# Depthwise taps of four channel blocks as shifted matmuls over (token parity, channel), the other four on VectorE, in a hybrid encoder trunk

## The chip, the core and the metric

One Trainium2 core runs the whole program; the other cores are idle. Its engines run side by side and meet at semaphores: TensorE (PE; its weight loads are listed apart as PEld), VectorE (DVE), ScalarE (ACT), GpSimd (POOL) and SyncE (SP), which issues the DMAs. The metric is device microseconds of one execution, lower is better. The kernel before was timed three times: 1600.88, 1602.43 and 1603.56 us, median 1602.43.

## What is computed

A trunk of four layers over one sequence of 256 tokens of 1024 channels, all in float32. Each layer has a token mixer (retention, Conformer convolution, dilated attention, retention again) and then a SwiGLU channel mixer, each between RMSNorms with a residual. The change touches the convolution mixer of layer 1:

```python
def _conv_mixer(h, w_in, b_in, w_dw, b_dw, ln_g, ln_b, w_out, b_out):
    a = h @ w_in + b_in
    u = a[..., :D_MODEL] * jax.nn.sigmoid(a[..., D_MODEL:])
    u = lax.conv_general_dilated(
        u, w_dw[:, None, :], window_strides=(1,), padding=[(15, 15)],
        dimension_numbers=('NWC', 'WIO', 'NWC'), feature_group_count=D_MODEL) + b_dw
    u = jax.nn.silu(_layernorm(u, ln_g, ln_b))
    return u @ w_out + b_out
```

The convolution is depthwise: each channel has its own 31 taps over time, and no channel sees another.

## The kernel before

The tokens lie in two tiles of 128 (t = 0, 1), the channels in eight blocks of 128 (cb). The order of the tokens within the tiles is a permutation that the host applies to input, masks and tables and takes back at the end: position p holds token 4 * (p mod 64) + p // 64, so each tile holds two of the four residues modulo 4.

Large products are split into a high and a low float32r part of both operands (`split`, L49: a cast on ACT, L50, and a subtraction on DVE, L51) and summed over three single-pass matmuls. Weights come in by SP's queue into one of seven `raw` buffers (`load_w`, L62, L64) and are split into `wh` and `wl` there. A buffer comes free when its reader has finished, and SP issues its DMAs in program order.

The convolution mixer (`conv`, L514) runs in these stages:

- `glu(t, c, ...)`: 24 matmuls of a projection (L183), scaled out of PSUM by ACT (`cab`, L534), transposed on TensorE to channels by tokens (L537), a sigmoid on ACT (L541), and the gating product on DVE (L544), which writes the tokens in their natural order into `upad`, 15 zeros on either side. It is called for (0,0), (0,1), (1,0), (0,2), (1,1), (0,3), (1,2), (1,3); call c gives the channel blocks 2c and 2c + 1.
- `taps(cb)`: the 31 taps of a block. By the table PE_TAPS, blocks 0, 2, 4 and 6 are done on DVE as one scaling (L559) and 30 multiply-adds over 256 tokens (L561). Blocks 1, 3 and 5 are done on TensorE: ACT builds a diagonal matrix for each tap (`dg`, L574), and an f32 matmul of 256 columns adds the shifted `upad` into a PSUM bank (L577). Of block 7 TensorE does seven taps and adds DVE's part of the rest through an identity (L585). ACT adds the bias and puts the tokens back in permuted order (`cvp`, L587).
- LayerNorm: transposes back to tokens by channels (L617), statistics (L620, L621), a reciprocal root on POOL (L112, L113), normalisation half on DVE (`yc`, L625) and half on ACT (L626), transposes (L634), affine and SiLU on ACT (`sy`, L637), and a split into `yh` and `yl`.
- The output product with conv_w_out (L200). Its first three weight blocks are split right behind the last tap on DVE (the `issue_after` at L605).

A scheduler places each instruction on its engine from an estimate of when its inputs will be there, so the order on an engine is not the order of the code.

## Time and profile before

| | |
|---|---|
| median of the three runs | 1602.43 us |
| the profiled execution's own time | 1601.92 us |
| its span, first to last instruction | 1600.1 us |
| PE busy | 1579.5 us, 99% of the span |
| DVE busy | 1046.6 us, 65% |
| ACT busy | 870.4 us, 54% |
| POOL busy | 71.7 us, 4% |
| moved by DMA | 274.27 MB, mean 171 GB/s |
| granted TensorE clock | 0.997 of full speed |

A row of a timeline gives the start, the length, the engine, the line of the kernel, the operation, output and inputs, how many instructions are merged, and in brackets the idle time before it and what ended it. The length of a merged row runs from its first start to its last end. An f32 matmul that accumulates shows as two instructions, so 100 of them count x200; transposes and float32r matmuls are one. Matmuls are pipelined, so one lasts longer than the distance to the next; that distance (the pitch) is what a stream costs. Line numbers are those of the kernel before unless said otherwise.

### The profile page before, as it was taken

The numbers are of one execution on the slowest core, as the hardware profiler recorded it, in microseconds if no ns is written. First come the engines' busy times: TensorE is split into PE (matmuls) and PEld (weight loads), VectorE is DVE, ScalarE is ACT, GpSimd is POOL, SyncE is SP. The second block draws the span as 40 slices with busy tenths as digits, with TensorE's granted clock in tenths as the row PEclk, the third lists the DMA queues.
The fourth block names the chain that finished last, engine by engine and source line by source line (L and its number), as shares of the span: only waits on it lengthen the run. The fifth ranks groups of instructions, "written<-read, shape, count | busy, mean of one in ns | idle before, by whom it ended". The sixth has DMA issues, their size and how long they took to land.

```text
span 1600.1 us, 21034 instructions
## 1 busy us (share of the span) xinstructions
PE 1579.5 (99%) x7742; PEld 1342.0 (84%) x7742; DVE 1046.6 (65%) x1594; ACT 870.4 (54%) x1392; POOL 71.7 (4%) x106
## 2 busy tenths in 40 slices
PE   9999999999999999999999999999999999999998
PEld 6888878888787888889999999888888888878886
DVE  7755684556697855467777877845567655675452
ACT  7544464545677654446666666745456444555441
POOL 1000010001000200010000000100010000010000
PEclk9999999999999999999999999999999999999999
DMA  8645475555303755444454444665655554576530
GB/s 314 231 139 192 148 241 189 189 206 180 127 1 132 263 177 210 156 139 159 130 155 151 148 146 159 214 207 175 209 179 168 183 168 131 163 237 202 193 119 27
DMA packets 79881, 274.27 MB, mean 171 GB/s; under 512 B 9377, under 2 KB 9633, under 8 KB 79778
## 3 DMA queue, kind: packets, MB, share of 16 engines
q1 hardware_dynamic: 79778, 272.92, 51.1%
q8 instruction: 61, 1.00, 0.3%
q14 instruction: 42, 0.34, 0.1%
HBM read 271.84 MB, written 1.05 MB: 171 GB/s over the span
## 4 chain that ended last, share of the span: by engine, by line
PE 89%; ACT 3%; DVE 3%; DMA 2%; issue 1%; POOL 1%; SPq 0%; DVEq 0%; POOLq 0%; ACTq 0%
PE mm L183 56%; PE acc L200 20%; PE acc L577 3%; PE acc L776 1%; PE aux L459 1%; PE aux L324 1%; ACT wh L50 1%; PE aux L761 1%; DMA raw<-in_ffn_w_out 1%; PE acc L735 1%; DMA raw<-in_ffn_w_in 1%; ACT junk L118 1%; DMA raw<-in_ret_w_in 1%; DVE wl L51 1%; PE acc L733 1%
## 5 line engine op out<-in xcount | busy, mean ns | idle before, releaser
L183 PE MATMUL mm<-wh,xTh 128*128 128x512 f32 (+1 forms) x1536 | 591.0, 385 | 1.1 <-ACT xTh L50 1.1
L183 PE MATMUL mm<-wh,xTl 128*128 128x512 f32 (+1 forms) x1536 | 579.3, 377 | 0.0
L183 PE MATMUL mm<-wl,xTh 128*128 128x512 f32 (+1 forms) x1536 | 579.2, 377 | 0.0
L51 DVE TENSOR_TENSOR wl<-raw,wh 128x1024 fp32r<-128x1024 f32 (+1 forms) x432 | 498.1, 1163 | 117.6 <-ACT wh L50 103.6
L50 ACT CAST wh<-raw 128x1024 fp32r<-128x1024 f32 (+1 forms) x432 | 429.9, 1004 | 138.8 <-PE mm L183 103.3
L183 PEld LDWEIGHTS mm<-wh,xTl 128*128 128x128 f32 x1536 | 288.6, 188 | 46.0 <-DVE xTl L51 0.3
L183 PEld LDWEIGHTS mm<-wh,xTh 128*128 128x128 f32 x1536 | 289.0, 188 | 43.3 <-ACT xTh L50 1.5
L183 PEld LDWEIGHTS mm<-wl,xTh 128*128 128x128 f32 x1536 | 289.4, 188 | 41.8 <-DVE wl L51 0.5
L448 ACT ACTIVATE fsg<-mm,rsx 128x256 f32<-128x256 f32 x88 | 41.7, 474 | 168.2 <-PE mm L183 168.2
L450 DVE SCALAR_TENSOR_TENSOR fsg<-mm,rsx,fsg 128x256 f32<-128x256 f32 x88 | 42.3, 481 | 123.6 <-ACT fsg L448 123.5
L51 DVE TENSOR_TENSOR pooll<-raw,poolh 128x1024 fp32r<-128x1024 f32 x88 | 107.3, 1222 | 7.5 <-ACT poolh L50 6.7
L200 PE MATMUL acc<-poolh,fhh 128*128 128x512 f32 x344 | 107.6, 393 | 0.5 <-ACT fhh L50 0.5
L200 PE MATMUL acc<-poolh,fhl 128*128 128x512 f32 x344 | 107.2, 392 | 0.0
L200 PE MATMUL acc<-pooll,fhh 128*128 128x512 f32 x344 | 106.0, 389 | 0.0
L50 ACT CAST poolh<-raw 128x1024 fp32r<-128x1024 f32 x88 | 92.6, 1054 | 23.7 <-PE acc L200 14.6
L51 DVE TENSOR_TENSOR fhl<-aux,fhh 128x256 fp32r<-128x256 f32 x88 | 37.1, 421 | 97.9 <-ACT fhh L50 97.9
L50 ACT CAST fhh<-aux 128x256 fp32r<-128x256 f32 x88 | 32.5, 369 | 114.8 <-PE aux L459 114.8
L200 PEld LDWEIGHTS acc<-poolh,fhh 128*128 128x128 f32 x344 | 63.7, 188 | 15.1 <-ACT fhh L50 2.7
L200 PEld LDWEIGHTS acc<-pooll,fhh 128*128 128x128 f32 x344 | 64.6, 188 | 13.5
L200 PEld LDWEIGHTS acc<-poolh,fhl 128*128 128x128 f32 x344 | 64.3, 188 | 13.5
L561 DVE SCALAR_TENSOR_TENSOR cv<-upad,wdw,cv 128x256 f32<-128x256 f32 x143 | 59.5, 478 | 0.8
L110 POOL TENSOR_SCALAR rs<-ss 128x1 f32<-128x1 f32 x16 | 7.6, 475 | 1040.5 <-ACT junk L118 1040.5
(180 smaller groups left out, 1622.0 us busy)
## 6 DMA issues: line engine op xcount, KB each, us to landing
raw<-in_ffn_w_in SPq DMA_DIRECT2D x176, 512.0 KB, 4.7
raw<-in_ret_w_in SPq DMA_DIRECT2D x96, 512.0 KB, 4.9
raw<-in_ffn_w_out SPq DMA_DIRECT2D x88, 512.0 KB, 4.7
raw<-in_attn_w_in SPq DMA_DIRECT2D x96, 384.0 KB, 3.7
raw<-in_ret_w_out SPq DMA_DIRECT2D x32, 512.0 KB, 4.5
raw<-in_conv_w_in SPq DMA_DIRECT2D x16, 512.0 KB, 4.7
gain<-in_norm_w SPq DMA_DIRECT2D x15, 512.0 KB, 5.5
raw<-in_conv_w_out SPq DMA_DIRECT2D x8, 512.0 KB, 4.5
```

The lines of the kernel that those rows point to most:

```text
L50: ia = nc.scalar.copy(h, src)
L51: iv = nc.vector.tensor_sub(l, src, h.bitcast(F32))
L118: nc.scalar.activation(junk, src, AF.Square, scale=scale, accum_out=acc)
L183: nc.tensor.matmul(out, lhsT=st[t][:, k, :], rhs=mv[:, sl], start=(n == 0), stop=(n == 23))
L200: nc.tensor.matmul(acc[hh], lhsT=st, rhs=mv[:, hh * 512 : hh * 512 + 512], start=(first and i == 0), stop=(last and i == 2),)
L324: nc.tensor.matmul(b, lhsT=pt[:, m, t * P : (t + 1) * P], rhs=vt[:, m, :], start=(n == 0), stop=(n == 5))
L448: nc.scalar.activation(sg, b[:, 0:256], AF.Silu, scale=rsx[t])
L450: nc.vector.scalar_tensor_tensor(out=sm, in0=b[:, 256:512], scalar=rsx[t], in1=sg, op0=ALU.mult, op1=ALU.mult)
L459: nc.tensor.transpose(tp[:, k * P : (k + 1) * P], sm[:, k * P : (k + 1) * P], ident)
L561: last_tap["v"] = nc.vector.scalar_tensor_tensor(out=cv, in0=upad[:, cb, w : w + 256], scalar=wdw[:, cb, w : w + 1], in1=cv, op0=ALU.mult, ...
L577: nc.tensor.matmul(pc[:, 0:256], lhsT=dgs[w], rhs=upad[:, cb, w : w + 256], start=(w == 0), stop=(w == TAPS - 1),)
L733: nc.tensor.matmul(b[:, 0:256], lhsT=x[:, 0, ts_(t)], rhs=y[:, h, :], start=(n == 0), stop=(n == 2))
```

## The change

The token order becomes by parity: position p holds token 2 * (p mod 128) + p // 128, so tile 0 holds the even tokens and tile 1 the odd ones.

Blocks 0 to 3 are all done on DVE, 31 taps each. For blocks 4 to 7 the gating product writes `su`, channels by tokens of one parity. Sixteen DMAs on POOL's queue copy halves of 64 channels into `uw`, whose 128 partitions are (token parity, 64 channels), for eight groups of 64 channels, 144 columns each, zeroed by a POOL memset. A convolution over 31 tokens is then 16 shifts by one pair of tokens: for each shift d a matmul takes the 128 columns of `uw` from d on as its stationary operand and, as its moving operand, a 128x128 matrix that maps (input parity, channel) to (output parity, channel); it holds the tap 2d + q - r on its diagonals. These matrices are made by the host (conv_tz, 8.4 MB) and come through the `raw` buffers, sixteen loads of 512 KB. The result is already tokens by channels, so these blocks aren't transposed back; their bias enters as two single-row matmuls per PSUM bank (`cbrh`, `cbrl`). The statistics are taken in four pieces of 256 channels, and ACT normalises its half in two strided pieces.

```diff
--- before.py
+++ after.py
@@ -30,8 +30,8 @@
 CONV_FENCE = 1
 APE = 3
 PTB = 1
-PE_TAPS = (0, 31, 0, 31, 0, 31, 0, 7)
-TAP_ORDER = (0, 1, 2, 3, 4, 5, 6, 7)
+VB = 4
+SHIFTS = 16
 
 
 @with_exitstack
@@ -518,14 +518,21 @@
         nc.sync.dma_start(wdw, a["conv_w_dw"][j])
         bout = pool.tile([P, D], F32, tag="cbout", name="cbout", bufs=1)
         nc.sync.dma_start(bout, a["conv_b_out"][j : j + 1, :].partition_broadcast(P))
-        upad = pool.tile([P, KB, 288], F32, tag="upad", name="upad", bufs=1)
+        brow = pool.tile([1, D], F32, tag="cbrow", name="cbrow", bufs=1)
+        nc.sync.dma_start(brow, a["conv_b_row"][j : j + 1, :])
+
+        upad = pool.tile([P, VB, 288], F32, tag="upad", name="upad", bufs=1)
         nc.vector.memset(upad[:, :, 0:15], 0.0)
         nc.vector.memset(upad[:, :, 271:288], 0.0)
-        cvp = pool.tile([P, KB, 256], F32, tag="cvp", name="cvp", bufs=1)
-
-        def perm(v):
-
-            return v.rearrange("p (u r) -> p r u", r=4)
+        cvp = pool.tile([P, VB, 256], F32, tag="cvp", name="cvp", bufs=1)
+
+        GR = 2 * (KB - VB)
+        su = pool.tile([P, KB - VB, 2, P], F32, tag="su", name="su", bufs=1)
+        uw = pool.tile([P, GR, 144], F32, tag="uw", name="uw", bufs=1)
+        nc.gpsimd.memset(uw, 0.0)
+        brh = pool.tile([1, D], F32R, tag="cbrh", name="cbrh", bufs=1)
+        brl = pool.tile([1, D], F32R, tag="cbrl", name="cbrl", bufs=1)
+        split(brh, brl, brow)
 
         def glu(t, c, ws, mid=None):
             b = bank("mm")
@@ -541,23 +548,32 @@
                 nc.scalar.activation(
                     sg, tp[:, (2 + k) * P : (3 + k) * P], AF.Sigmoid, bias=chv[:, 4, cb : cb + 1]
                 )
+                if cb < VB:
+                    dst = upad[:, cb, 15:271].rearrange("p (v t) -> p t v", t=2)[:, t, :]
+                else:
+                    dst = su[:, cb - VB, t, :]
                 nc.vector.scalar_tensor_tensor(
-                    out=perm(upad[:, cb, 15:271])[:, 2 * t : 2 * t + 2, :],
-                    in0=tp[:, k * P : (k + 1) * P].rearrange("p (r u) -> p r u", r=2),
+                    out=dst,
+                    in0=tp[:, k * P : (k + 1) * P],
                     scalar=chv[:, 3, cb : cb + 1],
-                    in1=sg.rearrange("p (r u) -> p r u", r=2),
+                    in1=sg,
                     op0=ALU.add,
                     op1=ALU.mult,
                 )
+                if cb >= VB:
+                    for q in range(2):
+                        lo = 64 * (1 - t)
+                        nc.gpsimd.dma_start(
+                            uw[lo : lo + 64, 2 * (cb - VB) + q, 7 + t : 135 + t],
+                            su[64 * q : 64 * q + 64, cb - VB, t, :],
+                        )
 
         last_tap = {}
 
         def taps(cb):
-            n = PE_TAPS[cb]
             cv = pool.tile([P, 256], F32, tag="cv", name="cv", bufs=2)
-            if n < TAPS:
-                nc.vector.tensor_scalar_mul(cv, upad[:, cb, n : n + 256], wdw[:, cb, n : n + 1])
-            for w in range(n + 1, TAPS):
+            nc.vector.tensor_scalar_mul(cv, upad[:, cb, 0:256], wdw[:, cb, 0:1])
+            for w in range(1, TAPS):
                 last_tap["v"] = nc.vector.scalar_tensor_tensor(
                     out=cv,
                     in0=upad[:, cb, w : w + 256],
@@ -566,30 +582,33 @@
                     op0=ALU.mult,
                     op1=ALU.add,
                 )
-            if n:
-                pc = bank("acc")
-                dgs = []
-                for w in range(n):
-                    dg = pool.tile([P, P], F32, tag="dg", name="dg", bufs=16)
-                    nc.scalar.activation(dg, ident, AF.Copy, scale=wdw[:, cb, w : w + 1])
-                    dgs.append(dg)
-                for w in range(n):
-                    nc.tensor.matmul(
-                        pc[:, 0:256],
-                        lhsT=dgs[w],
-                        rhs=upad[:, cb, w : w + 256],
-                        start=(w == 0),
-                        stop=(w == TAPS - 1),
-                    )
-                if n < TAPS:
-                    nc.tensor.matmul(pc[:, 0:256], lhsT=ident, rhs=cv, start=False, stop=True)
-                cv = pc[:, 0:256]
             last_tap["a"] = nc.scalar.activation(
-                cvp[:, cb, :].rearrange("p (r u) -> p r u", r=4),
-                perm(cv),
+                cvp[:, cb, :].rearrange("p (t v) -> p t v", t=2),
+                cv.rearrange("p (v t) -> p t v", t=2),
                 AF.Identity,
                 bias=chv[:, 0, cb : cb + 1],
             )
+
+        def windows(bk):
+
+            pc = bank("acc")
+            sl = slice(bk * 512, bk * 512 + 512)
+            for i, row in enumerate((brh, brl)):
+                nc.tensor.matmul(pc, lhsT=ones.bitcast(F32R), rhs=row[:, sl], start=(i == 0), stop=False)
+            for q in range(4):
+                for hf in range(2):
+                    tz = wp.tile([P, 1024], F32, tag="raw", name="raw", bufs=RAWBUFS)
+                    nc.sync.dma_start(tz, a["conv_tz"][j, 4 * bk + q, hf])
+                    for i in range(8):
+                        d = 8 * hf + i
+                        nc.tensor.matmul(
+                            pc[:, q * P : (q + 1) * P],
+                            lhsT=uw[:, 4 * bk + q, d : d + P],
+                            rhs=tz[:, i * P : (i + 1) * P],
+                            start=False,
+                            stop=(q == 3 and d == SHIFTS - 1),
+                        )
+            return pc
 
         wc = {}
         for c in range(4):
@@ -599,8 +618,9 @@
             if c:
                 glu(1, c - 1, wc[c - 1])
         glu(1, 3, wc[3])
-        for cb in TAP_ORDER:
+        for cb in range(VB):
             taps(cb)
+        pcs = [windows(bk) for bk in range((KB - VB) // 2)]
 
         with tc.issue_after(last_tap["v"].ins):
             wo = [load_w(a["conv_w_out"][j, k]) for k in range(CONV_EARLY)]
@@ -609,21 +629,29 @@
         with tc.issue_after(last_tap["a"].ins):
             nc.scalar.activation(warm[:, 0:1], nhalf, AF.Silu)
         for t in range(2):
-            bs = [bank("acc"), bank("acc")]
-            bn = work.tile([P, 2, 6], F32, tag="bn", name="bn", bufs=2)
-            ms = work.tile([P, 16], F32, tag="lnm", name="lnm", bufs=2)
+            bs = bank("mm")
+            bn = work.tile([P, 4, 6], F32, tag="bn", name="bn", bufs=2)
+            ms = work.tile([P, 8], F32, tag="lnm", name="lnm", bufs=2)
+            for k in range(VB):
+                nc.tensor.transpose(bs[:, k * P : (k + 1) * P], cvp[:, k, t * P : (t + 1) * P], ident)
+            parts = [pc.rearrange("p (g t c) -> p g t c", t=2, c=64)[:, :, t, :] for pc in pcs]
             for hh in range(2):
-                for k in range(4):
-                    nc.tensor.transpose(
-                        bs[hh][:, k * P : (k + 1) * P], cvp[:, 4 * hh + k, t * P : (t + 1) * P], ident
-                    )
-                nc.vector.bn_stats(bn[:, hh, :], bs[hh])
+                nc.vector.bn_stats(bn[:, hh, :], bs[:, hh * 256 : hh * 256 + 256])
+            for hh in range(2):
+                nc.vector.bn_stats(bn[:, 2 + hh, :], parts[hh])
             nc.vector.bn_aggr(ms[:, 0:2], bn)
             rs = rsqrt_mean(ms[:, 1:2], None, LN_EPS, scale=1.0)
             nc.vector.tensor_scalar(ms[:, 2:3], ms[:, 0:1], rs, -1.0, op0=ALU.mult, op1=ALU.mult)
             yc = pool.tile([P, D], F32, tag="yc", name="yc", bufs=1)
-            nc.vector.tensor_scalar(yc[:, 0:512], bs[0], ms[:, 0:1], rs, op0=ALU.subtract, op1=ALU.mult)
-            nc.scalar.activation(yc[:, 512:1024], bs[1], AF.Identity, scale=rs, bias=ms[:, 2:3])
+            nc.vector.tensor_scalar(yc[:, 0:512], bs, ms[:, 0:1], rs, op0=ALU.subtract, op1=ALU.mult)
+            for hh in range(2):
+                nc.scalar.activation(
+                    yc[:, 512 + 256 * hh : 768 + 256 * hh].rearrange("p (g c) -> p g c", c=64),
+                    parts[hh],
+                    AF.Identity,
+                    scale=rs,
+                    bias=ms[:, 2:3],
+                )
             h = const.tile([P, KB, P], F32R, tag=f"xTh{t}", name=f"yh{t}")
             l = const.tile([P, KB, P], F32R, tag=f"xTl{t}", name=f"yl{t}")
             for hh in range(2):
@@ -893,7 +921,7 @@
 
     f32 = np.float32
     pos = np.arange(256)
-    tok = 4 * (pos % 64) + pos // 64
+    tok = 2 * (pos % 128) + pos // 128
     c = {}
     c["x"] = inputs["x"].reshape(256, D)[tok].reshape(2, P, D)
     c["ident"] = np.eye(P, dtype=f32)
@@ -918,6 +946,20 @@
     c["conv_w_in"] = (
         w.reshape(n, 4, 2, P, 2, 4, 256).transpose(0, 5, 1, 3, 2, 4, 6).reshape(n, 4, 4, P, 1024)
     )
+
+    vc = VB * P
+    wd = inputs["conv_w_dw"][:, :, vc:].reshape(n, TAPS, -1, 64)
+    tz = np.zeros((n, wd.shape[2], SHIFTS, 2, 64, 2, 64), f32)
+    ch = np.arange(64)
+    for d in range(SHIFTS):
+        for q in range(2):
+            for r in range(2):
+                if 0 <= 2 * d + q - r < TAPS:
+                    tz[:, :, d, q, ch, r, ch] = wd[:, 2 * d + q - r]
+    c["conv_tz"] = (
+        tz.reshape(n, -1, 2, SHIFTS // 2, P, P).transpose(0, 1, 2, 4, 3, 5).reshape(n, -1, 2, P, 8 * P)
+    )
+    c["conv_b_row"] = np.repeat(inputs["conv_b_dw"][:, vc:].reshape(n, -1, 1, 64), 2, axis=2).reshape(n, -1)
     c["conv_w_dw"] = inputs["conv_w_dw"].reshape(n, TAPS, KB, P).transpose(0, 3, 2, 1)
     chv = [inputs[k].reshape(n, 1, KB, P) for k in ("conv_b_dw", "conv_ln_g", "conv_ln_b")]
     chv.append(inputs["conv_b_in"].reshape(n, 2, KB, P))
```

Where the instructions stand. TensorE, from the last matmul of the last projection (L183; `cab` is the projection on its way to the transpose, `dg` a diagonal weight, `raw` a block of conv_tz), before and then now:

```order
L183 MATMUL mm<-wh,xTl_3487 128x512
L577 MATMUL acc<-upad,dg 128x256 x2
L537 MATMUL aux<-ident,cab 128x128 x4
L577 MATMUL acc<-upad,dg 128x256 x98
L585 MATMUL acc<-cv,ident 128x256
L617 MATMUL acc<-ident,cvp 128x128 x16
L634 MATMUL aux<-ident,yc 128x128 x12
```

```order
L183 MATMUL mm<-wh,xTl_3496 128x512
L597 MATMUL acc<-cbrh,ones 128x512
L597 MATMUL acc<-cbrl,ones 128x512
L604 MATMUL acc<-raw,uw 128x128 x2
L544 MATMUL aux<-ident,cab 128x128 x4
L604 MATMUL acc<-raw,uw 128x128 x62
L597 MATMUL acc<-cbrh,ones 128x512
L597 MATMUL acc<-cbrl,ones 128x512
L604 MATMUL acc<-raw,uw 128x128 x64
L636 MATMUL mm<-ident,cvp 128x128 x8
L662 MATMUL aux<-ident,yc 128x128 x12
```

Two window matmuls stand ahead of the last projection's transposes, as two tap matmuls did; 128 window matmuls of 128 columns take the place of 100 of 256, and eight transposes back that of sixteen.

DVE, from the last gating writes (`upad` or `su`) to the normalisation (`lnm`, `yc`); `wl` is the low part of a block of conv_w_out, before and then now:

```order
L561 SCALAR_TENSOR_TENSOR cv<-upad,wdw,cv 128x256 x10
L544 SCALAR_TENSOR_TENSOR upad<-aux,chv,csg 128x2x64
L561 SCALAR_TENSOR_TENSOR cv<-upad,wdw,cv 128x256 x2
L544 SCALAR_TENSOR_TENSOR upad<-aux,chv,csg 128x2x64
L561 SCALAR_TENSOR_TENSOR cv<-upad,wdw,cv 128x256 x21
L559 TENSOR_SCALAR cv<-upad,wdw 128x256
L561 SCALAR_TENSOR_TENSOR cv<-upad,wdw,cv 128x256 x27
L559 TENSOR_SCALAR cv<-upad,wdw 128x256
L561 SCALAR_TENSOR_TENSOR cv<-upad,wdw,cv 128x256 x39
L51 TENSOR_TENSOR wl<-raw,wh 128x1024 x3
L620 BN_STATS bn<-acc 128x6 x3
L621 BN_AGGR lnm<-bn 128x2
```

```order
L555 SCALAR_TENSOR_TENSOR su<-aux,chv,csg 128x128
L577 SCALAR_TENSOR_TENSOR cv<-upad,wdw,cv 128x256 x5
L575 TENSOR_SCALAR cv<-upad,wdw 128x256
L577 SCALAR_TENSOR_TENSOR cv<-upad,wdw,cv 128x256 x54
L641 BN_STATS bn<-acc 128x6
L577 SCALAR_TENSOR_TENSOR cv<-upad,wdw,cv 128x256 x3
L51 TENSOR_TENSOR wl<-raw,wh 128x1024 x3
L639 BN_STATS bn<-mm 128x6 x2
L641 BN_STATS bn<-acc 128x6
L639 BN_STATS bn<-mm 128x6
L642 BN_AGGR lnm<-bn 128x2
```

Behind the last gating write 62 taps and one scaling stand where 87 and two stood; the three casts of conv_w_out still stand between the last tap and most of the statistics.

ACT, at the end of the taps (`cvp` is the result of a block, `wh` the high part of a block of conv_w_out), before and then now:

```order
L587 ACTIVATE cvp<-cv,chv 128x256
L574 ACTIVATE dg<-ident,wdw 128x128 x6
L587 ACTIVATE cvp<-acc,chv 128x256 x2
L610 ACT_TABLE_LOAD
L610 ACTIVATE warm<-nhalf 128x1
L626 ACTIVATE yc<-acc,lnm,rs 128x512
```

```order
L548 ACTIVATE csg<-aux,chv 128x128 x2
L585 ACTIVATE cvp<-cv,chv 128x256
L50 CAST wh<-raw 128x1024 x2
L585 ACTIVATE cvp<-cv,chv 128x256
L50 CAST wh<-raw 128x1024
L585 ACTIVATE cvp<-cv,chv 128x256
L630 ACT_TABLE_LOAD
L630 ACTIVATE warm<-nhalf 128x1
L648 ACTIVATE yc<-acc,lnm,rs 128x256 x2
```

The third cast of conv_w_out now stands ahead of the last block's `cvp`. On SP's queue one load of conv_tz takes the place of the first load of conv_w_out, and the other fifteen stand between the small loads of this layer and all eight loads of conv_w_out.

## The prediction

> **What bounds the kernel now.** I read the chain of waits first, then the timelines of the conv stage, engine by engine. The chain over the span:
>
> ```profile
> PE 89%; ACT 3%; DVE 3%; DMA 2%; issue 1%; POOL 1%; SPq 0%; DVEq 0%; POOLq 0%; ACTq 0%
> ```
>
> TensorE holds nearly all of it, so a microsecond saved on the chain in one stage should reach the end unless the next stage waits for something else. The chain across the part that changes (start us, length us, what):
>
> ```profile
> 403.16 0.31 POOL rs L110
> ...
> 440.20 5.48 PE mm L183 x24
> ...
> 450.79 0.86 PE acc L577 x4
> 451.65 0.57 PE aux L537 x4
> 452.22 42.32 PE acc L577 x196
> 494.55 0.43 PE acc L585 x2
> ...
> 495.45 1.89 DVE bn L620 x3
> 497.35 0.12 DVE lnm L621
> ...
> 498.41 0.21 DVE lnm L623
> 498.62 0.73 DVE yc L625
> 499.35 0.04 issue
> 499.39 0.67 PE aux L634 x4
> ```
>
> After the last projection TensorE alone sets the pace for 43.6 us: 100 tap matmuls, two hardware passes each (x200). Only then comes the LayerNorm (DVE bn). VectorE's share in the same stretch (start, length, idle time before it in brackets):
>
> ```profile
> 428.75 0.45 DVE L544 SCALAR_TENSOR_TENSOR upad<-aux,chv,csg 128x128 f32<-128x128 f32 x1
> ...
> 446.72 0.45 DVE L544 SCALAR_TENSOR_TENSOR upad<-aux,chv,csg 128x128 f32<-128x128 f32 x1
> ...
> 454.10 8.50 DVE L561 SCALAR_TENSOR_TENSOR cv<-upad,wdw,cv 128x256 f32<-128x256 f32 x21
> 462.52 0.35 DVE L559 TENSOR_SCALAR cv<-upad,wdw 128x256 f32<-128x256 f32 x1
> 462.79 10.90 DVE L561 SCALAR_TENSOR_TENSOR cv<-upad,wdw,cv 128x256 f32<-128x256 f32 x27
> 473.60 0.35 DVE L559 TENSOR_SCALAR cv<-upad,wdw 128x256 f32<-128x256 f32 x1
> 473.87 16.40 DVE L561 SCALAR_TENSOR_TENSOR cv<-upad,wdw,cv 128x256 f32<-128x256 f32 x39
> 490.18 3.49 DVE L51 TENSOR_TENSOR wl<-raw,wh 128x1024 fp32r<-128x1024 f32 x3
> 495.45 1.89 DVE L620 BATCH_NORM_STATS2 bn<-acc 128x6 f32<-128x512 f32 x3 [1.78 <-PE acc L617]
> ```
>
> VectorE is only 1.78 us behind: its taps end at 490.18, and three weight casts (3.49 us) then fill the time until TensorE's last tap. So both engines must get shorter here, and a cast that was free becomes visible once TensorE is early.
>
> **VectorE, after.** Order rows: behind the last gating write stand 62 taps and 1 scaling, where 87 and 2 stood. Before, 454.10 to 490.18 is 36.08 us; less two scalings at a 0.27 us pitch (462.52 to 462.79) that is 35.54/87 = 0.41 us a tap. After: 62 x 0.41 = 25.4, plus 0.27, plus one batch-norm row that now stands among the taps (half the elements of L620's, whose three take 1.89 us: 0.3 to 0.6, I take 0.4). The last three taps belong to one block, each waiting for the one before; such a run is dearer:
>
> ```profile
> 424.72 4.11 DVE L561 SCALAR_TENSOR_TENSOR cv<-upad,wdw,cv 128x256 f32<-128x256 f32 x8
> ```
>
> that is 4.11/8 = 0.51 us, so +0.3. The last gating write itself waits a little, since ACT now does one cvp (0.77 us, first row below) ahead of its sigmoid: +0.4. The taps end at 454.1 + 0.4 + 26.4 = **480.9**, the three casts at **484.4**.
>
> ```profile
> 486.26 0.77 ACT L587 ACTIVATE cvp<-cv,chv 128x256 f32<-128x256 f32 x1 [0.77 <-DVE cv L561]
> ...
> 416.60 1.05 ACT L50 CAST wh<-raw 128x1024 fp32r<-128x1024 f32 x1
> ```
>
> **TensorE, after.** Four bias matmuls (128x512 in one pass, 5.48/24 = 0.23 us: 0.9 us together) and 128 f32 matmuls of 128 columns, two passes each: 256 passes. No f32 matmul of 128 columns that accumulates is in the trace. The nearest rows, first of the pace, then of the weight loads:
>
> ```profile
> 452.06 42.49 PE L577 MATMUL acc<-upad,dg 128*128 128x256 f32 x196
> 494.82 1.93 PE L617 MATMUL acc<-ident,cvp 128*128 128x128 f32 x16
> ...
> 744.97 0.28 PE L733 MATMUL acc<-kah,aqh 128*128 128x256 f32 x1
> ...
> 745.56 0.28 PE L735 MATMUL acc<-kbh,aql 128*128 128x256 f32 x1
> ...
> L577 PEld LDWEIGHTS acc<-upad,dg 128*128 128x128 f32 x200 | 37.7, 189 | 5.3
> L617 PEld LDWEIGHTS acc<-ident,cvp 128*128 128x128 f32 x16 | 1.8, 140 | 0.1
> ```
>
> L577: (42.49 - 0.38)/195 = 0.216 us a pass of 256 columns. L617, the transposes, are the same shape as the new passes, f32 weights loaded each time and 128 f32 columns: (1.93 - 0.27)/15 = 0.111 us, half of L577, so the load hides. The single-pass matmuls of attention (six from 744.97, the sixth at 745.56) go at 0.118 with loads as long as L577's. Bounds: 0.111 below, 0.189 above (a whole load of L577 shown on every pass). I take 0.115, between the two rows of like stream length. The first four passes and the projection's transposes stay where they were (resume near 452.1): 452.1 + 0.5 + 252 x 0.115 = **481.6**. At 0.111 it is 480.6, at 0.118 482.3.
>
> By the Trainium skill ("TensorE: Matmul & The Clock Gate", section "Back-to-back issue gap") a stream of load and matmul pairs at 128 columns needs about 81 ns each where the isolated gap is about 56, 1.45 times. Put on 0.111 that estimates 0.16 a pass; the transposes, which are such pairs, do not show it.
>
> **The join.** ACT's last cvp starts at the last tap or after the third weight cast (1.05 us) that stands ahead of it on ACT, about 481.0 to 481.8; TensorE transposes eight blocks, 8 x 0.111 = 0.9, done by 482.7. That is inside VectorE's casts, which therefore set the LayerNorm's start: 484.4 against 495.45, **11.0 us** earlier. The statistics ahead of the first aggregate are four half-size rows (1.2 to 2.4 us; 1.5) against 1.89: 0.4 more. ACT's normalisation splits in two halves, covered by DVE's yc and four transposes. TensorE runs on half clock after the LayerNorm now:
>
> ```profile
> 502.50:508.00 5.50, 5.50 (x17) 4.43 (x16) 3.71 (x5) 5.50 (x9) 0.00 (x0) 0.52 0.07 7
> ```
>
> (PEclk 0.52.) It idled from 496.7 to 499.4; after, it idles about 482.7 to 488: the slow phase stays, I price the difference at 0, bounds -1 to +1.5.
>
> **Loads and queues.** Sixteen 512 KB weight loads (8.4 MB) join SP's queue ahead of all conv_w_out loads, in the same seven raw buffers.
>
> ```profile
> GB/s 314 231 139 192 148 241 189 189 206 180 127 1 132 263 177 210 156 139 159 130 155 151 148 146 159 214 207 175 209 179 168 183 168 131 163 237 202 193 119 27
> raw<-in_conv_w_in SPq DMA_DIRECT2D x16, 512.0 KB, 4.7
> chv<-in_conv_ch SPq DMA_DIRECT2D x1, 20.0 KB, 1.7
> ident<-in_ident SPq DMA_DIRECT2D x1, 64.0 KB, 4.1
> ```
>
> Slice 12 (1 GB/s) is this stage: the queue is empty, and seven loads land during the projections. The other nine are freed by TensorE at 16 passes, 1.84 us, each: 285 GB/s, under the 314 of the first slice, with seven buffers of slack. The third conv_w_out load is freed by the twelfth window block, near 474.5, and lands at 479.2 (+4.7); its ACT cast (1.0 us) stands ahead of the last cvp. That is free by 1 us; if it lands 3 us late, the LayerNorm starts about 1 us later. Later loads stand in the same relation to their casts as before.
>
> POOL gets 16 small DMAs (32 KB), none of which the trace has from POOL. The last four follow gating writes near 453 and 454 and are first read at 466. The ninth is the tight one: it follows the write that ends at 447.2, and the first window matmul, at 451.1, waits for it. Two such matmuls stand ahead of the last projection's transposes, behind which stand ACT's last sigmoids and VectorE's last gating writes, in order: whatever it is late, TensorE and VectorE both lose. Landing 1.7 to 4.1 us (chv, ident), and I allow 1 us of POOL time: 449.9 to 452.3, so 0 to 1.2 us late; I take **0.4**. POOL can be slowed by VectorE:
>
> ```profile
> 410.52 0.60 PE L162 MATMUL aux<-ident,xg 128*128 128x128 f32 x4
> ...
> 392.29 1.82 POOL L110 TENSOR_SCALAR rsx<-ss 128x1 f32<-128x1 f32 x1 [3.27 <-ACT junk L118]
> 394.20 2.83 POOL L113 TENSOR_TENSOR rsx<-rsx,nhalf 128x1 f32<-128x1 f32 x1
> 403.55 0.56 POOL L113 TENSOR_TENSOR rs<-rs,nhalf 128x1 f32<-128x1 f32 x1
> ```
>
> The same operation took 0.56 and 2.83 us, the long one beside VectorE's weight casts. The Trainium skill's "SBUF — State Buffer", "Who interferes with whom", says a VectorE operation with two SBUF inputs blocks only those POOL instructions that read SBUF, and infers that descriptor writing is not among them; no run here shows it.
>
> The uw memset (1152 a partition) stands on POOL ahead of the second token tile's rsqrt at 403.16; that tile is first transposed at 410.52 (L162 above): of the 7.3 us between I estimate half as used by its products, so 3 us are covered. The bias row's split (1.0 us ACT, 1.2 us DVE) falls where ACT built diagonal weights, and the transposes that it could delay stand five matmuls (1.1 us) later: 0, at worst 1. The 100 diagonal builds leave ACT: 0 to -1, an estimate.
>
> **Sum.** 11.0 + 0.4 - 0.4 = 11.0 us. From the profiled execution, 1601.92 (span 1600.1 and 1.8 around it): 1590.9; from the median, 1602.43, half a microsecond above it: **1591.4**.
>
> **Rivals.**
> A, part of the gain: POOL needs 2.83 us a DMA (its longest row). Eight DMAs follow the gating writes from 429.2 on; with the short gaps between these the ninth is issued by 455.5 and lands at 457.5, 6.4 us late, for TensorE and VectorE alike: LayerNorm 490.8, gain 5, 1597.4. For: the row above. Against: it reads SBUF.
> B, no change: half or more of a load shows, (0.111 + 0.189)/2 = 0.15 to 0.178 a pass; at 0.16 the windows end at 452.6 + 40.3 = 492.9, the statistics start at 494: gain 1.5 to 2, 1600.5. For: loads of 0.189 are longer than a pass; against: the transposes. The Trainium skill's rule quoted above would put it here.
> C, slower: f32 weight loads don't hide behind 128 columns, 0.189 a pass: windows end at 452.6 + 47.6 = 500.2, statistics at 501.2 against 495.45, +5.8: 1608. It decides from (494.2 - 452.6)/252 = 0.165 a pass on. For: L577's loads are 189 ns against the transposes' 140, so they may not be the same load. Against: attention's 0.118.
> D, slower: POOL needs over 3.5 us a DMA, by which the ninth (429.2 + 9 x 3.5 + 2 = 462.7) is over 11.4 us late; at 4.5 it is 20.6 us late, 1612.
>
> **How the numbers follow.** Forecast 0.72, own range 1589 to 1594.5 (the join +-1, the ninth DMA -0.4 to +0.8, clock and loads +-1.5). A 0.12, B 0.05, C 0.07, D 0.04. Within 0.2% (3.2 us, about what a measurement of this kernel can tell) is B: 0.05. Faster is the forecast and A: 0.84; slower C and D: 0.11. The range from 1588 to 1602 leaves C, D and a larger gain out.
>
> **What would show it.** The window matmuls start every 0.11 to 0.12 us and end at 480.5 to 482.5; the last tap ends near 481; the three casts stand between it and the first statistics at 484 to 485; the first L200 of conv_w_out follows near 491. Wrong if the window passes go at 0.16 or more, if TensorE waits for uw ahead of the last projection's transposes by more than 1 us, if ACT's last cvp stands behind a late conv_w_out cast, or if the stages behind 530 keep their old times.

## The result, and the profile after

The changed kernel takes 1592.26 us (median of 4 runs, 1591.52 to 1593.72), the kernel before 1602.86 us (4 runs of the same comparison, 1600.88 to 1603.56). The ratio is 0.9937, 95% interval 0.992 to 0.9954: faster by 10.6 us, where 11.0 were forecast (1591.4). The profiled execution took 1592.03 us (span 1590.3), 9.9 less than that of before.

The chain that ended last, by engine (part 4 of the page of the changed kernel), and then its pieces in the conv stage (start us, length us, what):

```profile
PE 87%; DVE 5%; ACT 3%; DMA 3%; issue 2%; POOL 0%; SPq 0%; DVEq 0%; POOLq 0%; ACTq 0%
```

```profile
450.94 0.66 PE acc L597 x2
...
456.81 21.38 DVE cv L577 x54
...
479.87 3.49 DVE wl L51 x3
483.36 0.67 DVE bn L639 x2
...
486.04 0.73 DVE yc L646
```

Before, TensorE's tap matmuls filled 42 us of the chain here. Now the chain goes through VectorE: its taps, then the subtractions of the three weight casts (wl L51 x3), then the statistics (bn). That is the order that the prediction gave. (L597 are the bias matmuls; they come up again below.) TensorE's timeline in the same stretch (start, length, the idle time before in brackets):

```profile
451.53 0.71 PE L604 MATMUL acc<-raw,uw 128*128 128x128 f32 x4
...
452.51 14.01 PE L604 MATMUL acc<-raw,uw 128*128 128x128 f32 x124
...
467.11 14.56 PE L604 MATMUL acc<-raw,uw 128*128 128x128 f32 x128
481.51 1.04 PE L636 MATMUL mm<-ident,cvp 128*128 128x128 f32 x8
486.81 1.97 PE L662 MATMUL aux<-ident,yc 128*128 128x128 f32 x8 [4.27 <-DVE yc L646]
...
490.68 1.20 PE L200 MATMUL acc<-wh,yh 128*128 128x512 f32 x2
```

The windows (L604) end and the transposes of cvp (L636) follow without a break; those are done at 482.55. Then TensorE idles 4.27 us for VectorE. VectorE's timeline:

```profile
456.72 21.46 DVE L577 SCALAR_TENSOR_TENSOR cv<-upad,wdw,cv 128x256 f32<-128x256 f32 x54
478.11 0.42 DVE L641 BATCH_NORM_STATS2 bn<-acc 128x6 f32<-128x256 f32 x1
478.45 1.50 DVE L577 SCALAR_TENSOR_TENSOR cv<-upad,wdw,cv 128x256 f32<-128x256 f32 x3
479.87 3.49 DVE L51 TENSOR_TENSOR wl<-raw,wh 128x1024 fp32r<-128x1024 f32 x3
483.28 0.75 DVE L639 BATCH_NORM_STATS2 bn<-mm 128x6 f32<-128x256 f32 x2
...
485.95 0.80 DVE L646 TENSOR_SCALAR yc<-mm,lnm,rs 128x512 f32<-128x512 f32 x1
```

Up to the row at 483.28 no idle time stands in brackets: VectorE does not wait on its way to the statistics, so it sets their start, 483.28 (before: 495.45). From the program's start to this stage the executions of this study differ by up to 3.5 us, so I compare them from a zero of their own: the start of the last projection matmul of the conv stage (L183), at 450.40 us before and 450.56 after. From there, in us, read off the traces (a difference of two rounded rows can be off by 0.01):

| kernel | first yc of the LayerNorm | first L200 of conv_w_out | first L183 of the FFN |
|---|---|---|---|
| before | 48.14 | 52.10 | 78.25 |
| changed | 35.40 | 40.13 | 66.75 |
| e1, three subtractions late | 33.94 | 38.03 | 66.91 |
| e2, changed, idle stretch filled | 35.40 | 39.78 | 64.50 |
| e3, 16 taps fewer | 34.01 | 38.75 | 65.36 |
| e4, half of the windows | 35.28 | 40.01 | 66.84 |
| e5, before with the order alone | 48.14 | 52.09 | 76.99 |
| e6, POOL copies twice | 35.37 | 40.10 | 66.91 |
| e7, before, idle stretch filled | 48.14 | 52.11 | 76.03 |
| e8, filled, one subtraction late | 34.26 | 39.58 | 64.85 |
| e9, the same, another place | 34.27 | 38.64 | 62.81 |
| e10, windows plus half | 48.24 | 52.96 | 80.03 |
| e11, changed again | 35.40 | 40.13 | 66.41 |

The first column repeats to 0.03 us between executions of like kernels (48.14 three times; 35.37 to 35.40 four times), so tenths can be read from it where whole times scatter by 2 us and more. The gain is 12.7 us at the LayerNorm, 12.0 at conv_w_out and 11.5 at the FFN: some of it is given back on the way.

### The profile page after: what moved, and what is told of

Read it like the earlier page. It is cut to its first block, busy times and chain, and to the rows that moved or that the text cites. A ratio compares the mean times of both kernels' runs of the same rounds, so it can differ in the third digit from the quotient of the medians.

```text
span 1590.3 us, 21093 instructions
## 1 busy us (share of the span) xinstructions
PE 1565.7 (98%) x7792; PEld 1332.6 (84%) x7792; DVE 1036.6 (65%) x1575; ACT 834.2 (52%) x1291; POOL 83.3 (5%) x123
## 4 chain that ended last, share of the span: by engine, by line
PE 87%; DVE 5%; ACT 3%; DMA 3%; issue 2%; POOL 0%; SPq 0%; DVEq 0%; POOLq 0%; ACTq 0%
PE mm L183 57%; PE acc L200 20%; DVE cv L577 2%; PE acc L804 1%; PE aux L459 1%; DMA raw<-in_ffn_w_out 1%; PE aux L324 1%; DVE wl L51 1%; ACT wh L50 1%; PE aux L789 1%; PE acc L763 1%; DMA raw<-in_ret_w_in 1%; PE acc L761 1%; PE aux L300 1%; PE aux L728 1%
## 5 line engine op out<-in xcount | busy, mean ns | idle before, releaser
L183 PE MATMUL mm<-wh,xTh 128*128 128x512 f32 (+1 forms) x1536 | 591.1, 385 | 1.1 <-ACT xTh L50 1.1
L183 PE MATMUL mm<-wl,xTh 128*128 128x512 f32 (+1 forms) x1536 | 579.7, 378 | 0.0
L183 PE MATMUL mm<-wh,xTl 128*128 128x512 f32 (+1 forms) x1536 | 579.2, 377 | 0.0
L51 DVE TENSOR_TENSOR wl<-raw,wh 128x1024 fp32r<-128x1024 f32 (+1 forms) x432 | 497.9, 1163 | 118.2 <-ACT wh L50 104.0
L183 PEld LDWEIGHTS mm<-wh,xTl 128*128 128x128 f32 x1536 | 288.7, 188 | 45.9 <-DVE xTl L51 0.3
L183 PEld LDWEIGHTS mm<-wh,xTh 128*128 128x128 f32 x1536 | 289.1, 188 | 43.5 <-ACT xTh L50 1.5
L183 PEld LDWEIGHTS mm<-wl,xTh 128*128 128x128 f32 x1536 | 289.5, 188 | 41.7 <-DVE wl L51 0.5
L51 DVE TENSOR_TENSOR pooll<-raw,poolh 128x1024 fp32r<-128x1024 f32 x88 | 107.2, 1222 | 6.9 <-ACT poolh L50 6.2
L200 PE MATMUL acc<-poolh,fhh 128*128 128x512 f32 x344 | 107.6, 393 | 0.5 <-ACT fhh L50 0.5
L200 PE MATMUL acc<-poolh,fhl 128*128 128x512 f32 x344 | 107.2, 392 | 0.0
L200 PE MATMUL acc<-pooll,fhh 128*128 128x512 f32 x344 | 106.1, 389 | 0.0
L51 DVE TENSOR_TENSOR fhl<-aux,fhh 128x256 fp32r<-128x256 f32 x88 | 37.0, 421 | 97.9 <-ACT fhh L50 97.9
L200 PEld LDWEIGHTS acc<-poolh,fhh 128*128 128x128 f32 x344 | 63.7, 188 | 15.1 <-ACT fhh L50 2.7
L200 PEld LDWEIGHTS acc<-pooll,fhh 128*128 128x128 f32 x344 | 64.6, 188 | 13.5
L200 PEld LDWEIGHTS acc<-poolh,fhl 128*128 128x128 f32 x344 | 64.3, 188 | 13.5
L577 DVE SCALAR_TENSOR_TENSOR cv<-upad,wdw,cv 128x256 f32<-128x256 f32 x120 | 49.0, 478 | 0.1
```

The lines of the kernel that those rows point to most:

```text
L51: iv = nc.vector.tensor_sub(l, src, h.bitcast(F32))
L183: nc.tensor.matmul(out, lhsT=st[t][:, k, :], rhs=mv[:, sl], start=(n == 0), stop=(n == 23))
L200: nc.tensor.matmul(acc[hh], lhsT=st, rhs=mv[:, hh * 512 : hh * 512 + 512], start=(first and i == 0), stop=(last and i == 2),)
L577: last_tap["v"] = nc.vector.scalar_tensor_tensor(out=cv, in0=upad[:, cb, w : w + 256], scalar=wdw[:, cb, w : w + 1], in1=cv, op0=ALU.mult, ...
```

## The experiments

**Does VectorE set the join?** Four runs turn on this. The first takes 16 taps from VectorE:

```diff
-            for w in range(1, TAPS):
+            for w in range(1, TAPS - 8 if cb >= 2 else TAPS):
```

> The changed kernel without the last eight taps of the third and the fourth block on VectorE (16 of its 124 taps are left out, so the convolution of these two blocks is not the whole one). Theory (VectorE sets the join, TensorE is 1.2 us behind): taps end 16 x 0.395 = 6.3 us earlier, but the statistics start only 1.0 to 1.3 us earlier, at TensorE's transposes (482.0 to 482.3). Rival (TensorE's windows already set the join): statistics unmoved. Rival (the windows are slowed by VectorE's taps): window passes shorter than 0.112 us and the statistics 2 us or more earlier.

The timelines of this run, VectorE first, then TensorE:

```profile
479.15 2.46 DVE L51 TENSOR_TENSOR wl<-raw,wh 128x1024 fp32r<-128x1024 f32 x2 [1.60 <-ACT wh L50]
481.52 0.43 DVE L641 BATCH_NORM_STATS2 bn<-acc 128x6 f32<-128x256 f32 x1
481.87 1.08 DVE L639 BATCH_NORM_STATS2 bn<-mm 128x6 f32<-128x256 f32 x3
```

```profile
475.78 5.52 PE L604 MATMUL acc<-raw,uw 128*128 128x128 f32 x48
481.14 1.04 PE L636 MATMUL mm<-ident,cvp 128*128 128x128 f32 x8
```

The taps end 6.3 us earlier, the yc only 1.4 us (34.01 against 35.40). VectorE's taps do set the join, but what stops the gain here is not TensorE alone: the subtractions now wait for ACT's casts (3.07 us ahead of the first, 1.60 ahead of the second), the last gives way to the statistics at 481.52, and TensorE's windows end 0.2 us before that (475.78 + 5.52 = 481.30). The wait on TensorE by itself shows in e1 below, where the subtractions are out of the way. The windows keep their pitch, (5.52 - 0.28)/47 = 0.111 us a pass, though VectorE runs no tap beside them, so the taps do not slow them. One execution, 1590.36 us.

The other side, half of the window matmuls left out:

```diff
-                    for i in range(8):
+                    for i in range(0, 8, 2) if (q, hf) != (3, 1) else (0, 2, 4, 7):
```

> The changed kernel with half of the window matmuls (64 of 128; all loads kept; the other 64 shifts are left out of the convolution of the four blocks). Theory (VectorE sets the join): TensorE is done 64 x 0.224 = 14.3 us earlier, yet the statistics still start where the taps and the three casts end, 483.3, within 0.5 us; the time is that of the changed kernel within 1 us, 1591 to 1593.5. Rival (TensorE sets it): the statistics start 1 to 3.5 us earlier.

TensorE is free 14 us earlier and waits for the last cvp twice (7.42 and 1.69 us, in TensorE's timeline), and the yc stands where it stood, 35.28 against 35.40:

```profile
477.22 0.69 PE L636 MATMUL mm<-ident,cvp 128*128 128x128 f32 x2 [7.42 <-ACT cvp L585]
479.60 0.69 PE L636 MATMUL mm<-ident,cvp 128*128 128x128 f32 x2 [1.69 <-ACT cvp L585]
```

One execution, 1591.46 us. And 64 window matmuls more:

```diff
-                    for i in range(8):
+                    for i in (0, 1, 2, 3, 0, 1, 2, 3, 4, 5, 6, 7):
```

> The changed kernel with the first four shifts of every block of eight issued twice (192 instead of 128 window matmuls; the repeated shifts count twice, so the convolution is another one). Theory (a two-pass window matmul of 128 columns costs 0.224 us whatever else runs, TensorE has 1.2 us to spare at the join): the windows end 64 x 0.224 = 14.3 us later, the statistics start near 496, 13 us later than in the changed kernel, time 1604 to 1606. Rival (the pitch of 0.224 us held only beside VectorE's taps and loads as they are, or the tile's loads set it): more or less than that by 2 us or more.

```profile
473.91 21.70 PE L604 MATMUL acc<-raw,uw 128*128 128x128 f32 x192
495.45 1.04 PE L636 MATMUL mm<-ident,cvp 128*128 128x128 f32 x8
```

(TensorE's timeline.) The pass stays at (21.70 - 0.28)/191 = 0.112 us, and the yc is 12.84 us later: 14.3 of added work, less a slack of 1.5, which e1 below finds too (1.46). One execution, 1604.59 us; here TensorE decides. Together with e1 the runs agree on one picture: both engines work in parallel up to the join, VectorE is 1.5 us behind, and beyond that a microsecond of TensorE costs a microsecond.

**Are the casts a part of it?** The prediction said that three casts of conv_w_out stand between the last tap and the statistics. They can go behind:

```diff
+                nc.scalar.copy(wh, raw)
+                late.append((raw, wh, wl))
...
-            nc.vector.tensor_scalar(yc[:, 0:512], bs, ...)
+            cen = nc.vector.tensor_scalar(yc[:, 0:512], bs, ...)
+            if t == 0:
+                with tc.issue_after(cen.ins):
+                    for raw, wh, wl in late:
+                        nc.vector.tensor_sub(wl, raw, wh.bitcast(F32))
```

> The changed kernel with one edit: the three low-part subtractions of the early conv_w_out blocks (3.49 us of VectorE between its last tap and the LayerNorm statistics) are issued behind the first token tile's centring instead. Theory (VectorE's taps and these three set the join): the statistics start when TensorE's first four transposes are done, at 482.0 to 482.3 on the changed kernel's scale instead of 483.28, and the first yc moves up as much, 1.0 to 1.3 us. The second tile's statistics, yc and the split of yh then stand behind the subtractions, so at most this 1.2 us shows in the whole time: 1591 to 1592.5. Rival (TensorE's windows set the join): statistics and time unmoved, or slower by up to 1 us because the subtractions come late for conv_w_out.

The yc comes 1.46 us earlier: now VectorE waits for the end of TensorE's windows ahead of its statistics (VectorE's timeline):

```profile
481.51 0.43 DVE L649 BATCH_NORM_STATS2 bn<-acc 128x6 f32<-128x256 f32 x1 [1.75 <-PE acc L604]
```

The first L200 comes 2.1 us earlier, but the FFN no earlier (66.91 against 66.75); time 1591.79 us (1591.18 to 1592.89), ratio to before 0.9935 (0.9919 to 0.9952), which is not told apart from the changed kernel. Where it went (TensorE's waits between 497 and 520 us, then VectorE's timeline):

```profile
PE acc L200 <- ACT yh L50: 2.0, 1, 2.0
```

```profile
485.02 3.48 DVE L658 TENSOR_TENSOR wl<-raw,wh 128x1024 fp32r<-128x1024 f32 x3
...
491.02 8.04 DVE L51 TENSOR_TENSOR wl<-raw,wh 128x1024 fp32r<-128x1024 f32 x7
...
499.10 0.80 DVE L654 TENSOR_SCALAR yc<-mm,lnm,rs 128x512 f32<-128x512 f32 x1
```

With three subtractions ahead of it the second token tile is overtaken by all seven later casts; its yc ends 10 us later than in the changed kernel and TensorE runs out of work for 2.0 us in conv_w_out. So the casts do stand on the path, as predicted, and the wait was moved, not removed.

**What does the half clock cost?** TensorE's granted clock by stretches of the changed kernel (columns: stretch, its length, busy time of PE, PEld, DVE, ACT and POOL, PEclk, DMA share, GB/s), and of the kernel before:

```profile
482.00:484.50 2.50, 0.54 (x5) 0.30 (x3) 2.50 (x6) 0.04 (x1) 0.00 (x0) 1.00 0.88 269
484.50:490.60 6.10, 2.63 (x11) 2.26 (x12) 3.85 (x11) 3.65 (x10) 1.49 (x4) 0.50 0.79 306
490.60:494.80 4.20, 4.20 (x14) 3.32 (x13) 2.62 (x4) 4.20 (x8) 0.00 (x0) 0.50 0.00 1
```

```profile
496.00:501.00 5.00, 1.84 (x15) 1.37 (x13) 3.66 (x10) 2.68 (x6) 1.48 (x4) 1.00 0.30 116
501.00:502.50 1.50, 0.85 (x4) 0.71 (x4) 0.43 (x2) 1.50 (x5) 0.00 (x0) 0.50 0.00 0
```

The half clock lasts 10.2 us after the change (484.55 to 494.79 in the clock record) and 6.8 before (500.99 to 507.82); in e11, another execution of the changed kernel, it lasts 6.8 too. Does that shift the comparison? Both kernels were run with the idle stretch filled by matmuls that nobody reads (17 in the changed kernel, 10 in the one before, in the way shown):

```diff
+        fill = bank("aux")
+        for i in range(FILL):
+            nc.tensor.matmul(fill, lhsT=wo[0][0][:, 0:P], rhs=wo[0][0][:, 0:512],
+                             start=(i == 0), stop=(i == FILL - 1))
```

> The changed kernel with 17 extra matmuls of 512 columns whose result nobody reads, put on TensorE between the transposes ahead of the LayerNorm and those behind it; the eight transposes of both token tiles are written ahead of the loop for this. Nothing else moves in any engine's order. Theory (the idle stretch of 4.3 us is what costs the half clock from 484.6 to 494.8): with the stretch filled (17 x 0.228 = 3.9 us) the transposes behind yc take 0.9 us instead of 1.97 and the first L200 matmuls 0.23 instead of 0.43, the first FFN matmul comes 2 to 3 us earlier, time 1589 to 1590.5. Rival (the half clock follows the time of the program, not the idle stretch, or conv_w_out then waits for its casts): 0, 1591.5 to 1593; if the extra matmuls run at half clock they delay yc's transposes and cost up to 3 us.

> The kernel before with ten extra matmuls of 512 columns, whose result nobody reads, in TensorE's idle stretch ahead of the LayerNorm's transposes (2.65 us there). Theory (the half clock cost both kernels about the same, so the comparison of the two is not shifted by it): the first L200 matmuls run at 0.23 us instead of 0.43 to 0.53 each, 2 to 3 us earlier at the FFN, time 1599.5 to 1600.5. Rival (the half clock cost the kernel before less, and the change lost a part of its gain to it): 1601.5 to 1602.5.

TensorE's timeline in e2:

```profile
482.37 4.11 PE L637 MATMUL aux<-wh 128*128 128x512 f32 x17
486.52 1.09 PE L667 MATMUL aux<-ident,yc 128*128 128x128 f32 x8
...
490.04 0.70 PE L200 MATMUL acc<-wh,yh 128*128 128x512 f32 x2
```

The clock stays full through this stage in both runs; in e2 the eight transposes take 1.09 us instead of 1.97, the first pair of L200 0.70 instead of 1.20. The FFN comes 2.25 us earlier than in the changed kernel (64.50 against 66.75) and 2.22 us earlier than in the one before (76.03 against 78.25). Times: e2 1590.62 us (1588.56 to 1593.32), ratio 0.9927 (0.9911 to 0.9942); e7 1600.93 us (1600.17 to 1603.44), ratio 0.999 (0.9981 to 1.0). Both medians lie a little above their forecast ranges, and whole times alone tell neither gain safely from none; the FFN's start in the profiled executions does. The cost is the same on both sides though one half-clock spell is 3.4 us longer, and the rows above show where the longer spell goes: in its first 6.1 us TensorE is busy for 2.63 only and waits for the rest. The change is worth 11.5 us at the FFN with and without it.

**The token order alone.** In the kernel before, with its taps as they were:

```diff
-            return v.rearrange("p (u r) -> p r u", r=4)
+            return v.rearrange("p (u r) -> p r u", r=2)
...
-    tok = 4 * (pos % 64) + pos // 64
+    tok = 2 * (pos % 128) + pos // 128
```

> The kernel before with the token order alone changed: parity (even tokens, odd tokens) instead of four residues; taps, diagonal matmuls and everything else as before. Theory (the order only lets the windows be built; the gain is work taken from TensorE and VectorE): no change within 1.5 us of the kernel before; the gating writes get shorter (0.35 instead of 0.45 us, 16 of them) but stand off the path. Rival (a part of the 10 us is the order, by shorter gating writes that bring the taps forward): 1598 to 1600.

1602.15 us (10 runs, 1600.66 to 1604.34) against 1603.04: ratio 0.9994 (0.9984 to 1.0003). The yc stands at 48.14, to the hundredth where it was, and so does the first L200 to 0.01. No gain of the order by itself shows; its FFN came 1.3 us earlier in the profiled execution, and what differs there between the traces is the half clock, which lasted 3.4 us instead of 6.8.

**The copies on POOL.** The prediction took the ninth copy into uw for tight.

```diff
-                    for q in range(2):
+                    for q in (0, 0, 1, 1):
```

> The changed kernel with every POOL copy into uw issued twice (32 instead of 16, the same bytes to the same place). Theory (a copy costs POOL 0.52 us and lands 1.7 us later, so the ninth had about 2 us to spare): the eighth pair ends in time and the windows start within 0.5 us of their old place; time within 1 us of the changed kernel, 1591 to 1593.5. Rival (the ninth copy is tight, as the prediction had it): the windows start 2 us or more later and the time is 1594 or more.

POOL's timeline of the changed kernel, then of this run, then the latter's row of DMA issues:

```profile
447.52 1.03 POOL L566 DMA_DIRECT2D uw<-su  x2 [3.86 <-DVE su L555]
```

```profile
447.96 4.11 POOL L566 DMA_DIRECT2D uw<-su  x8 [1.23 <-DVE su L555]
```

```profile
uw<-su POOLq DMA_DIRECT2D x32, 32.0 KB, 1.7
```

A copy costs POOL 4.11/8 = 0.51 us, and half of them land within 1.7 us of their issue, also with twice as many; the slowest takes 4.0 us in the changed kernel and 5.0 here. The yc stands at 35.37; one execution, 1592.56 us. But the run does not test the ninth copy as was meant, since the edit also changed TensorE's order. No window stands ahead of the last projection's transposes (L544) any more; all 128 start behind them, 1.94 us after the zero instead of 0.97:

```profile
452.44 0.65 PE L544 MATMUL aux<-ident,cab 128*128 128x128 f32 x4
452.94 28.75 PE L604 MATMUL acc<-raw,uw 128*128 128x128 f32 x256
```

That the ninth copy was not tight is shown by the changed kernel itself. It is issued at 447.52 and lands 1.7 us later, near 449.2; the first window starts at 451.53, right behind the bias matmuls and without a wait, 2.3 us behind the landing. The slow copies, 2.9 to 4.0 us, are the last four, issued from 453.82 on and not read before the second bank's windows at 467.11.

**A better version.** Two gains are on the table: 2.2 us of clock and 1.2 to 1.5 us of casts. e8 fills the stretch with 13 matmuls and puts only the third subtraction behind the first centring, where it does not push the second tile behind the later casts:

```diff
+            wo = [load_w(a["conv_w_out"][j, k]) for k in range(CONV_EARLY - 1)]
+            late = []
+            for k in range(CONV_EARLY - 1, CONV_EARLY):
...
```

> The changed kernel with 13 extra matmuls in the idle stretch, and the subtraction of the third early conv_w_out block alone put behind the first token tile's centring (e1 put all three there). Theory (VectorE ends 1.2 us behind TensorE's transposes, one subtraction is 1.16 us; the half clock costs 2.3 us; the two add up, since one subtraction does not delay the second tile beyond its old place): yc 1.2 us earlier than in the run with 17 extra matmuls, first FFN matmul 3.4 us earlier than in the changed kernel, time 1588.5 to 1590. Rival (the second tile is late again, as with all three): the 1.2 us is given back in a wait on the second tile's yh, 1590.5 to 1591.5.

1589.53 us (1588.92 to 1590.21), ratio 0.9916 (0.9902 to 0.9931). The yc is 1.14 us earlier, as forecast, but L200 only 0.2 us against e2, and the FFN is 0.35 us later than there: 1.9 us ahead of the changed kernel where 3.4 were expected. So the rival's wait came, and that the whole time fell into the range of the theory is luck. TensorE's timeline shows why:

```profile
489.51 0.63 PE L680 MATMUL aux<-ident,yc 128*128 128x128 f32 x4 [2.99 <-DVE yc L660]
```

The third group of four transposes belongs to the second token tile and stands ahead of L200 in TensorE's order; it waits 2.99 us for that tile's yc, which the subtraction delayed. After that wait the clock halved again, for 3.4 us of L200 (490.51 to 493.93 in the clock record). In e9 the subtraction stands behind the split of yh:

```diff
                     with tc.issue_after(ends[0].ins), tc.issue_after(ends[1].ins):
+                        for raw, wh, wl in late:
+                            nc.vector.tensor_sub(wl, raw, wh.bitcast(F32))
                         wo += [load_w(a["conv_w_out"][j, k]) for k in range(CONV_EARLY, KB)]
```

> As e8 (13 extra matmuls, the third early subtraction late), but the subtraction stands behind the first token tile's second split of yh instead of behind its centring. Theory (in e8 TensorE's next four transposes, which wait for the second tile's yc, came 1.2 us later than they could, since the subtraction stood ahead of that tile's statistics): the second tile's yc ends near 488.1, the first L200 starts 1.2 us earlier than in e2 and e8, and the FFN 3.3 us earlier than in the changed kernel; time 1588.3 to 1589.5. Rival (conv_w_out's third block is then late by as much): a wait on wl of 0.5 to 1.2 us among the L200 matmuls, time 1589.5 to 1590.5.

TensorE's timeline of e9, and VectorE's:

```profile
487.73 0.63 PE L676 MATMUL aux<-ident,yc 128*128 128x128 f32 x4 [2.04 <-ACT yh L50]
488.11 0.70 PE L200 MATMUL acc<-wh,yh 128*128 128x512 f32 x2
```

```profile
486.78 0.80 DVE L660 TENSOR_SCALAR yc<-mm,lnm,rs 128x512 f32<-128x512 f32 x1
...
490.31 1.22 DVE L694 TENSOR_TENSOR wl<-raw,wh 128x1024 fp32r<-128x1024 f32 x1
```

1587.11 us (1586.36 to 1588.85), ratio to before 0.9903 (0.989 to 0.9917): 15.4 us under the kernel before. For the direct comparison the changed kernel ran again on the same chip:

> The changed kernel unaltered, for the comparison with the kernel of e9 on one chip: 1591.5 to 1593.5.

1592.52 us (5 runs, 1590.12 to 1596.28), ratio 0.9933 (0.9919 to 0.9946). e9 is 5.4 us below it by the medians; at the FFN 3.94 us are shown (62.81 against 66.75; 3.6 against e11), 0.6 more than expected. The 5.4 us, and a median under the forecast range, hold a part that the edit does not explain: of the 5.6 us between the two profiled spans (1584.7 and 1590.3), 1.1 us lie ahead of the common zero and 0.5 behind the FFN's start. L200 starts 1.14 us earlier than in e2, and no wait for wl stands among its matmuls, so the rival for e9 falls.

## Why the prediction was right, step by step

- **The bound, and what bounds after.** Right. TensorE's 43.6 us gave way to VectorE's taps and casts (e1, e3, e4), with TensorE close behind (e10).
- **VectorE, 480.9 and 484.4.** The taps ended at 479.95, the casts at 483.3: 1.1 us too late in the forecast, 1.3 counted from the common zero, which stands 0.16 us later in this execution. The term that was mis-sized is 62 x 0.41: the 54 taps in one row go at (21.46 - 0.5)/53 = 0.395 us, which makes 0.9 us. The 0.41 was a mean that already held a run of dependent taps: in the old kernel's rows, 21 taps from 454.10 to 462.52 are 0.401 each, but the last 39, from 473.87 to 490.18, are 0.418. The prediction then added 0.3 for its own dependent taps, and so counted such a run twice. Those three took 1.50 (3 x 0.50), the batch-norm row 0.42 (0.4 taken). Of the 0.4 for the last gating write 0.1 came (454.36 - 0.16 against 454.10). Its reason did not hold: the sigmoid ahead of it waited for TensorE's transposes, not for ACT's cvp, which took 0.53 us instead of 0.77.
- **TensorE, 0.115 a pass, 481.6.** (14.01 - 0.28)/123 = 0.112 us, inside the bounds and next to the transposes' 0.111, which were the right row to trust. The windows ended near 481.7. The load of the weights is long in the record and hidden in the pace (groups of line L604: shortest, median, longest ns):

```profile
L604 PEld LDWEIGHTS acc<-raw,uw x256: 186/192/192, 451.5 to 481.3; 128*128 128x128 f32 x128
L604 PE MATMUL acc<-raw,uw x256: 275/275/377, 451.5 to 481.4; 128*128 128x128 f32 x128
```

  A load of 192 ns every 112 ns: neither B (0.15 and more) nor C (0.165 and more) has a place here. The rule weighed in the prediction, the Trainium skill's "TensorE: Matmul & The Clock Gate", section "Back-to-back issue gap", would by the estimate made there have put a pass at 0.16; this trace does not agree with it for two-pass f32 matmuls, at 0.112. The four bias matmuls took 0.33 us each in this trace instead of 0.23, 0.4 us together (in e6, where all four stand in a row, the middle two take 0.24 and 0.23). The second two had no effect, since TensorE had 1.5 us of slack. The first two stand ahead of the last projection's transposes and so on the chain (450.94 above); there the last gating write but one comes 0.3 us later, mostly for it (453.18 - 0.16 against 452.72). The last comes 0.1 later, since behind the one before it the order now has a scaling in place of a second tap.
- **The join, 11.0 + 0.4.** 12.7 us from the common zero. The 0.4 for the shorter statistics is there: 2.67 us from the first bn to the first yc (483.28 to 485.95) against 3.09.
- **The ninth copy, 0.4 late.** Not late at all (451.53, without a wait). Landing in 1.7 us was taken as the lower bound and held for this copy; of the 1 us allowed for POOL it took half. A and D, which rested on slow copies, fall with it. A copy takes 0.51 to 0.52 us on POOL while VectorE's taps run, against the 2.83 us of the row on which A rested, a POOL operation that reads SBUF. That agrees with the Trainium skill's "SBUF — State Buffer", section "Who interferes with whom": a VectorE operation with two SBUF inputs blocks only those POOL instructions that read SBUF, and it infers that descriptor writing is not among them.
- **The clock, priced at 0.** Right: 2.2 us on both sides (e2, e7; one profiled execution each).
- **uw's memset, the bias row's split, the loads of the shift weights.** The memset took 1.06 us and the loads 4.6; no wait of TensorE in the stage names any of them. Hidden, as priced. The third load of conv_w_out was closer than priced: its ACT cast ran from 478.99 to 480.03, the last tap ended at 479.95, so of the 1 us to spare nothing was left once the taps came early.
- **What the sum left out.** At the first yc it had 11.0 (11.0 + 0.4 - 0.4), and 12.7 came: 0.9 from the pitch of the taps, 0.4 from the copy, 0.3 from the last gating write, 0.1 in small pieces. Then 1.2 us were given back between yc and FFN, which no step of the prediction has. On full clock the way from yc to L200 takes 4.38 us after the change (e2) and 3.97 before (e7): the second tile's first four transposes stand ahead of L200 in TensorE's order, and that tile's yc now starts 3.05 us behind the first (489.00 after 485.95) instead of 2.06 (500.60 after 498.54), since two of its statistics rows stand between. In nine of the ten executions of the changed kernel and its variants those transposes start 0.15 us behind the end of that yc (in e1, whose second tile comes far later, 1.36 us). This is the split statistics' other side; the prediction counted only the first tile. The other 0.8 us lie between L200 and the FFN (24.72 us in e2, 23.92 in e7). A part shows in waits on VectorE around the end of conv_w_out (waits of TensorE, 500 to 517.3 us after, 511 to 528.6 before: total, times, longest), 0.5 us more after than before; the rest stays open:

```profile
PE aux L162 <- DVE xg L141: 0.4, 1, 0.4
PE acc L200 <- DVE yl L51: 0.3, 1, 0.3
```

```profile
PE aux L162 <- DVE xg L141: 0.2, 1, 0.2
```

So the total came out within a microsecond partly by luck, because two errors of opposite sign met: 1.7 us too little at the join, 1.2 us not given back. The condition named as a sign of error, that the stages behind 530 keep their old times, did not come: the FFN starts 11.5 us earlier. At the end of the profiled execution 9.9 are left. From the FFN's start to the end the three traces with the old taps take 1071.5 to 1072.5 us and nine with the new ones 1072.0 to 1073.5 (e11 1075.2), so most of that difference is scatter; a small loss in later stages is not ruled out.

## What to carry to other kernels

Where two engines end within a microsecond or two of each other, cost both to the join and list everything that stands in line between the last real work and the join; a cast that was hidden is on the path as soon as the other engine gets faster. Moving such a piece behind the join is worth something only if the next work that is queued behind it has the time: e1 lost all of its 2 us, e9 kept it by moving one piece of three to a place where nobody waits. And compare stages from an event shortly ahead of the change, not from the program's start: the join repeats to 0.03 us while whole executions scatter by 2 to 6 us.
